# A hybrid decoder layer in split float32: weight chunks taken in pairs, and another order of the three partial products

## The chip, the cores and the metric

The kernel runs on one core of one Trainium2 chip. The metric is the device time of one execution in microseconds (us). An execution is also recorded by the profiler; the views quoted here come from that trace. Engines: TensorE (PE, its weight loads shown apart as PEld), VectorE (DVE), ScalarE (ACT), GpSimd (POOL) and SyncE (SP, which issues the weight transfers).

## The reference

One layer for 256 tokens of width 2048: half a SwiGLU, a token mixer, half a SwiGLU, each between two RMS norms. DEPTH is 1 and D_FF is 5504.

```python
def swiglu(x, w_gate, w_up, w_down):
    return (jax.nn.silu(x @ w_gate) * (x @ w_up)) @ w_down

f1 = swiglu(rms_norm(h, ffn1_pre_norm[l]), ffn1_w_gate[l], ffn1_w_up[l], ffn1_w_down[l])
h = h + 0.5 * rms_norm(f1, ffn1_post_norm[l])
m = hybrid_token_mixer(rms_norm(h, mix_pre_norm[l]), l, w_in[l], ..., w_out[l])
h = h + rms_norm(m, mix_post_norm[l])
f2 = swiglu(rms_norm(h, ffn2_pre_norm[l]), ffn2_w_gate[l], ffn2_w_up[l], ffn2_w_down[l])
h = h + 0.5 * rms_norm(f2, ffn2_post_norm[l])
```

The mixer multiplies its input by `w_in`, runs two gated linear attentions (GLA and HGRN2) on slices of the result, multiplies their outputs by two branch matrices, adds them under gates, and multiplies the sum by `w_out`. All arrays are float32.

## The kernel before, in words

**Products.** Tokens lie in two tiles of 128 (`NT`, index t); the contraction runs in k tiles of 128: 16 for a width of 2048 (`KT`), 43 for 5504 (`FKT`). Every float32 operand is split into a float32r part `hi` and a rest `lo`, and a product of two operands is three matmuls into one PSUM bank (`mm3`): hi*hi, then the activation's hi with the weight's lo, then the activation's lo with the weight's hi. The activation is the stationary operand (`xhi`, `xlo`, or `hkhi`, `hklo` in the second product of an FFN), the weight (`whi`, `wlo`, 512 columns) streams.

**Weight chunks.** `wchunk` brings 512 KB of a weight by one transfer on SP's queue into a tile `raw`, ACT writes `hi` (line 119), and DVE subtracts it from `raw` and writes `lo` (line 120). Tiles `raw`, `whi` and `wlo` have four buffers each, taken in turn, so the next transfer or split waits until the fourth one back is no longer read. Each engine takes its instructions in the order in which the tile framework laid them out. A chunk holds two k tiles by 512 columns in `gemm_block`, and one k tile by 1024 columns (half `hf` of the 2048) in `out_proj`; either is used for 12 matmuls.

**gemm_block** makes 512 columns for both token tiles. Without `held`, it takes a chunk, lays its products for t = 0 and t = 1, calls `side.pump()`, and goes on. The first block of each sublayer has `held`: there chunks are kept and token tile 1 follows as a whole; the change leaves that branch alone.

**out_proj** makes all 2048 columns in eight PSUM banks (four column blocks n by two t). The first four chunks are (k tile 0, half 0), (1, 0), (0, 1), (1, 1); then come half 0 and half 1 of each further k tile up to the last four (`TAIL`). Those last four give eight chunks at once, the four of half 0 in the ring and the four of half 1 in tiles `held`; they are used group by group, so that one (t, n) after the other is finished. `finish` then does the norm, the residual, and the next sublayer's transposed operand.

**Side work.** `Side.pump` lays one step of each waiting chain (transposes, attention, `finish`) between the products.

Of the kernel before, what the change touches and what calls it, by code (L numbers as in the profile page):

```python
# [16 lines left out]
D = 2048  # L17
NT = 2
# [13 lines left out]
class Side:  # L32
    """Chains of small steps whose instructions are laid between those of the large products.

    A light chain takes one step at every pump, the heavy ones take turns; a chain yields
    where the tensor engine would have to wait for what the other engines were just given."""

# [13 lines left out]
    def pump(self):  # L51
        for g in list(self.light):
            self._step(self.light, g)
        if self.heavy:
            g = self.heavy.pop(0)
            # two at a time take turns
            self.heavy.insert(min(1, len(self.heavy)), g)
            self._step(self.heavy, g)
# [12 lines left out]
def kernel(ctx: ExitStack, tc: tile.TileContext, a: dict, out: bass.AP):  # L71
    nc = tc.nc
    side = Side()
# [24 lines left out]

    # ------------------------------------------------------------------ weights
    def ring_alloc(w):  # L100
# [4 lines left out]
    def wchunk(src: bass.AP, w: int, alloc=ring_alloc):  # L105
        """src: [128, 2, w] of a weight in DRAM -> the float32r parts (hi, lo) of its two halves."""
        raw = ring.tile([P, 2, w], F32, tag="raw", name=nm("raw"))
        nc.sync.dma_start(raw, src)
        parts = alloc(w)
        if len(parts) == 1:  # L110
            split_into(*parts[0], raw)
            hi, lo = parts[0]
            return [(hi[:, i, :], lo[:, i, :]) for i in range(2)]
        for i, (hi, lo) in enumerate(parts):
            split_into(hi, lo, raw[:, i, :])
        return parts
# [5 lines left out]
    def mm3(ps, x, w, start, stop):  # L122
        (xhi, xlo), (whi, wlo) = x, w
        nc.tensor.matmul(ps, lhsT=xhi, rhs=whi, start=start, stop=False)  # L124
        nc.tensor.matmul(ps, lhsT=xhi, rhs=wlo, start=False, stop=False)  # L125
        nc.tensor.matmul(ps, lhsT=xlo, rhs=whi, start=False, stop=stop)  # L126

    def gemm_block(w_dram, c0, w, lhs, nkt=KT, held=None):
        """[256, w] of x @ W, one bank a token tile (two halves in two banks if w > 512). With
        held, the chunks after the ring's stay in its tiles, and token tile 1 comes after all  # L130
        of token tile 0."""
        nb = -(-w // CB)
        pss = [[ps_tile(f"mm{t}") for _ in range(nb)] for t in range(NT)]

        def chunk(k0, alloc):
            return wchunk(w_dram[k0 * P:(k0 + 2) * P, c0:c0 + w].rearrange("(k p) c -> p k c", p=P),
                          w, alloc)

        def mm(t, k0, parts):
            for i, part in enumerate(parts):  # L140
                kt = k0 + i
                x = lhs(t, kt)
                for j, ps in enumerate(pss[t]):
                    sl = slice(j * (w // nb), (j + 1) * (w // nb))
                    mm3(ps[:, :w // nb], x, (part[0][:, sl], part[1][:, sl]),
                        kt == 0, kt == nkt - 1)

        if held is None:
            for k0 in range(0, nkt, 2):
                parts = chunk(k0, ring_alloc)  # L150
                for t in range(NT):
                    mm(t, k0, parts)
                side.pump()
        else:
            kept = []
            for i, k0 in enumerate(range(0, nkt, 2)):
                kept.append((k0, chunk(k0, ring_alloc if i < 4 else held)))
                mm(0, *kept[-1])
                side.pump()
            for k in kept:  # L160
                mm(1, *k)
                side.pump()
            side.flush()
        return pss if nb > 1 else [ps[0] for ps in pss]

    # ------------------------------------------------------------------ helpers
    def load_bcast(name, after):
        """A row of 2048 on every partition, in four tiles; not before `after` is issued."""
        ts = []
# [7 lines left out]
    def rstd(ss, n, width, tag):  # L177
        """(ss / n + eps) ** -0.5 for ss [128, width]."""
        v = small.tile([P, width], F32, tag=f"{tag}v", name=nm("v"))
# [17 lines left out]
    def lhs_of(x):  # L197
        def lhs(t, kt):
            # the products are laid behind the transposes that they read
            side.until(lambda: x[2][t] > kt)  # L200
# [3 lines left out]
    def to_T(x, t, n, src):  # L204
        """src [128 tokens, 512] -> k tiles 4n.. of x's token tile t."""
        ps = ps_tile()
# [5 lines left out]
    def rstd4(ss, scale, tag):  # L212
        """rstd of rows of D whose squares' sums are in the four columns of ss; all but the
        last column is added up beforehand. scale: a power of two, into the result."""
        c = 1.0 / (D * scale * scale)
# [14 lines left out]
    def first_norm(t, x, rs, wcol):  # L230
        """x's token tile t = (h * w) transposed, the weights one channel a partition."""
        if t:
# [20 lines left out]
    def out_proj(w_dram, nkt, lhs, post, scale, pre, held, after):  # L253
        """acc = lhs @ W [256, 2048]; h += scale * rmsnorm(acc) * post; then the next
        sublayer's transposed operand (h * pre, and the rows' rstd, applied later), or the
        kernel's output."""
        acc = [[None] * 4 for _ in range(NT)]
        wpost = load_bcast(post, after)
        early, nxt, rs = [], None, [None, None]
        if pre is not None:  # L260
            # h * pre + rstd * acc * (post * pre): all but the second product ahead of time
            wpre = load_bcast(pre, after)
# [17 lines left out]
        for i, (kt, hf) in enumerate(order):  # L280
            parts = load(kt, hf)
            for t in range(NT):
                for n in (2 * hf, 2 * hf + 1):
                    mm(t, n, kt, parts)
            if i == 1:
# [12 lines left out]
        def finish(t, ss):  # L298
# [6 lines left out]
            if pre is None:  # L305
                # GpSimd takes one of the four
                for n in range(4):
# [46 lines left out]

    # ------------------------------------------------------------------ FFN
    def ffn(pre, x, rs, post, pre_next):
# [49 lines left out]

    # ------------------------------------------------------------------ mixer
    def mixer(x, rs):
        xl = lhs_of(x)
        w_in = a["w_in"]  # L410
        with ExitStack() as mctx:
# [11 lines left out]

            # masks of the small levels' pairs, four heads wide, and of the diagonal
            diag = mp.tile([P, P], U8, name="diag")
# [8 lines left out]

            # lower bounds of the HGRN forget gates: softmax over the two rows of logits,
            # one head a column
            lg = blk("lg")
# [34 lines left out]
            def transposed(src, dst):  # L472
                """A step later, dst = src with each 128 columns transposed."""
                yield
# [21 lines left out]
            def spawn_T(srcs, s):  # L496
                """Transposes of the two token tiles' blocks, a step later."""
                dsts = []
# [5 lines left out]
            def attention(t, qT, kT, fT, vs, gates, dv, br, b0):  # L504
                """Four heads of 128 key channels on token tile t; fT: the decays. kT holds
                each key times the decays after it in its block, qT each query times those up
                to it; from level to level the blocks double, and the pairs of a block's halves
                get their scores, as products of two factors in [0, 1]."""
                sc = blk("sc")
# [11 lines left out]
                for lv, c in enumerate(LEVELS):  # L521
# [11 lines left out]
                    else:  # L533
                        # the blocks' rectangles lie on the engine's own borders
                        for r0 in range(0, P, 2 * c):
# [99 lines left out]
            def gla_decays(code, fT):  # L635
                """exp(logsigmoid(code @ w + b) / 16), transposed; logsigmoid(y) as
                min(y, 0) - ln(1 + exp(-|y|))."""
                cs = blk("code")
# [76 lines left out]

            # ---- HGRN2, four heads at a time
            for g in range(2):
# [15 lines left out]

            # ---- gated merge
            ms = []
# [87 lines left out]
```

## Time and profile before

| | |
|---|---|
| time, median of 3 runs | 2231.12 us (2229.8 to 2231.39) |
| span of the profiled execution | 2230.0 us (no other time of that execution is given) |
| instructions | 26331 |
| mean granted TensorE clock | 0.997 |
| busy ACT, POOL | 45%, 3% |
| DMA | 410.24 MB, mean 184 GB/s |

The span runs from the first to the last instruction on the core. A timeline row gives start, duration, engine, line, operation, output from inputs, and in brackets the engine's idle time just before with the one it waited for. A matmul's duration is longer than the distance to the next one, since matmuls overlap; the distance of the starts is what counts. A wait row names engine, tile and line, what it waited for, the total in us, the number of times and the longest.

### The profile page before, as it was taken

Reading aid. Unit: us, or ns where it says so; the run is one execution under the profiler, and the core shown is the slowest. Engines: PE = TensorE matmul, PEld = TensorE weight load, DVE = VectorE, ACT = ScalarE, POOL = GpSimd, SP = SyncE. Lnnn points to the kernel's source line nnn. Section 1 sums busy time; section 2 is a strip of 40 time slices with the busy share of each in tenths; the row PEclk is TensorE's granted clock in tenths of the full one; section 3 lists DMA queues with packets and bytes.
Section 4 is the critical chain, followed back from the end, with each engine's and each line's share of the span. In section 5 each row is a group of like instructions: output and inputs, shape, how many; then the busy total and the mean of one; then the engine's idle time right before and its main releaser. Section 6 shows DMA issues by size and latency. Waiting matters only on the chain.

```text
span 2230.0 us, 26331 instructions
## 1 busy us (share of the span) xinstructions
PE 2203.5 (99%) x10197; PEld 1816.2 (81%) x10197; DVE 1183.0 (53%) x1278; ACT 995.1 (45%) x1202; POOL 69.1 (3%) x106
## 2 busy tenths in 40 slices
PE   8999999999999999999999999999999999999998
PEld 6888888898888788888888888878888888898886
DVE  5544444446555744657575656465444444445554
ACT  5444444444444564444434444355444444444443
POOL 0000000000000400000000000021000000000001
PEclk9999999999999999999999999999999999999999
DMA  7666666666666556655556775555666666666664
GB/s 233 186 187 185 189 186 185 189 200 205 190 192 196 159 171 189 170 148 145 155 154 174 232 204 185 183 171 177 188 189 186 184 188 189 170 217 190 191 193 135
DMA packets 189344, 410.24 MB, mean 184 GB/s; under 512 B 13681, under 2 KB 22289, under 8 KB 189218
## 3 DMA queue, kind: packets, MB, share of 16 engines
q1 hardware_dynamic: 183712, 400.21, 60.6%
q10 hardware_dynamic: 5506, 8.34, 1.2%
q8 instruction: 80, 1.31, 0.2%
q14 instruction: 46, 0.38, 0.0%
HBM read 406.41 MB, written 2.10 MB: 183 GB/s over the span
## 4 chain that ended last, share of the span: by engine, by line
PE 64%; DVE 1%; POOL 1%; ACT 0%; issue 0%; DMA 0%; POOLq 0%; ACTq 0%
PE mm L124 16%; PE mm L126 16%; PE mm L125 16%; PE acc L125 5%; PE acc L126 5%; PE acc L124 5%; PE ps L187 1%; PE ps L531 1%; PE ps L581 0%; PE ps L538 0%; POOL h L303 0%; PE ps L515 0%; DVE tmp L295 0%; DMA raw<-in_ffn_w_down_dram 0%; POOL v L218 0%
## 5 line engine op out<-in xcount | busy, mean ns | idle before, releaser
L120 DVE TENSOR_TENSOR wlo<-raw,whi 128x1024 fp32r<-128x1024 f32 (+2 forms) x740 | 898.4, 1216 | 889.3 <-ACT whi L119 888.3
L119 ACT ACTIVATE whi<-raw 128x1024 fp32r<-128x1024 f32 (+2 forms) x740 | 777.1, 1051 | 1072.5 <-PE mm L126 800.5
L124 PE MATMUL mm<-whi,xhi 128*128 128x512 f32 (+2 forms) x2096 | 817.0, 390 | 3.6 <-ACT whi L119 3.6
L125 PE MATMUL mm<-wlo,xhi 128*128 128x512 f32 (+2 forms) x2096 | 809.6, 386 | 5.0 <-DVE wlo L120 5.0
L126 PE MATMUL mm<-whi,xlo 128*128 128x512 f32 (+2 forms) x2096 | 810.0, 386 | 0.0
L125 PEld LDWEIGHTS mm<-wlo,xhi 128*128 128x128 f32 x2096 | 394.7, 188 | 84.6 <-DVE wlo L120 6.2
L124 PEld LDWEIGHTS mm<-whi,xhi 128*128 128x128 f32 x2096 | 394.2, 188 | 83.0 <-ACT whi L119 4.0
L126 PEld LDWEIGHTS mm<-whi,xlo 128*128 128x128 f32 x2096 | 394.0, 188 | 81.1 <-DVE xlo L120 0.7
L125 PE MATMUL acc<-wlo,hkhi 128*128 128x512 f32 x656 | 257.6, 393 | 0.3 <-DVE wlo L120 0.3
L124 PE MATMUL acc<-whi,hkhi 128*128 128x512 f32 x656 | 257.2, 393 | 0.5 <-ACT hT L376 0.5
L126 PE MATMUL acc<-whi,hklo 128*128 128x512 f32 x656 | 257.5, 393 | 0.0
L125 PEld LDWEIGHTS acc<-wlo,hkhi 128*128 128x128 f32 x656 | 123.2, 188 | 29.2 <-DVE wlo L120 1.3
L124 PEld LDWEIGHTS acc<-whi,hkhi 128*128 128x128 f32 x656 | 123.2, 188 | 28.7 <-ACT hT L376 1.0
L126 PEld LDWEIGHTS acc<-whi,hklo 128*128 128x128 f32 x656 | 123.1, 188 | 27.7
L217 POOL TENSOR_TENSOR v<-ss 128x1 f32<-128x1 f32 x12 | 6.3, 524 | 1691.7 <-ACT sq L228 1690.8
L124 PE MATMUL mm<-whi,oT 128*128 128x512 f32 x128 | 51.3, 401 | 0.0
L126 PE MATMUL mm<-whi,oT 128*128 128x512 f32 x128 | 50.7, 396 | 0.0
L125 PE MATMUL mm<-wlo,oT 128*128 128x512 f32 x128 | 50.6, 395 | 0.0
L119 ACT ACTIVATE hkhi<-hT 128x512 fp32r<-128x512 f32 (+1 forms) x44 | 26.9, 621 | 52.2 <-PE acc L125 52.1
L120 DVE TENSOR_TENSOR hklo<-hT,hkhi 128x512 fp32r<-128x512 f32 (+1 forms) x44 | 29.6, 679 | 31.0 <-ACT hkhi L119 31.0
L125 PE MATMUL acc<-wlo,xhi 128*128 128x512 f32 x112 | 44.1, 394 | 0.0
L126 PE MATMUL acc<-whi,xlo 128*128 128x512 f32 x112 | 44.0, 393 | 0.0
(196 smaller groups left out, 1145.0 us busy)
## 6 DMA issues: line engine op xcount, KB each, us to landing
raw<-in_ffn_w_down_dram SPq DMA_DIRECT2D x172, 512.0 KB, 4.5
raw<-in_w_in_dram SPq DMA_DIRECT2D x168, 512.0 KB, 3.8
raw<-in_ffn_w_gate_dram SPq DMA_DIRECT2D x160, 512.0 KB, 3.8
raw<-in_ffn_w_up_dram SPq DMA_DIRECT2D x160, 512.0 KB, 3.6
raw<-in_w_out_dram SPq DMA_DIRECT2D x32, 512.0 KB, 4.1
raw<-in_w_branch_gla_dram SPq DMA_DIRECT2D x16, 512.0 KB, 3.6
raw<-in_w_branch_hgrn_dram SPq DMA_DIRECT2D x16, 512.0 KB, 3.8
raw<-in_ffn_w_gate_dram SPq DMA_DIRECT2D x16, 384.0 KB, 3.3
```

The lines of the kernel that those rows point to most:

```text
L119: nc.scalar.activation(hi, src, AF.Copy)
L120: nc.vector.tensor_tensor(lo, src, hi.bitcast(F32), op=ALU.subtract)
L124: nc.tensor.matmul(ps, lhsT=xhi, rhs=whi, start=start, stop=False)
L125: nc.tensor.matmul(ps, lhsT=xhi, rhs=wlo, start=False, stop=False)
L126: nc.tensor.matmul(ps, lhsT=xlo, rhs=whi, start=False, stop=stop)
L187: nc.tensor.transpose(dst_ps[:, i * P:(i + 1) * P], src[:, i * P:(i + 1) * P], ident)
L217: nc.gpsimd.tensor_tensor(v[:, 0:1], ss[:, 0:1], ss[:, 1:2], op=ALU.add)
L531: nc.tensor.matmul(ps[:, i * 64:(i + 1) * 64], lhsT=kT[:, sl], rhs=halves(qT[:, sl])[1], start=True, stop=True)
```

## The change

Three edits. In `gemm_block` without `held`, two chunks are fetched together (four k tiles), and for each token tile the products go in the order of k tiles 2, 0, 1, 3: the second chunk's first k tile, both of the first chunk, the second chunk's other one. `side.pump()` is called after each token tile, as often as before. In `out_proj`, behind the first four chunks, the two halves of a k tile are fetched together, half 0 first, and half 1 is used first. In `mm3` the second and third matmul change places: hi*hi, the activation's lo with the weight's hi, then the activation's hi with the weight's lo. The output is the same sum in another order. Line numbers move by 3 to 10 behind line 136.

```diff
     def mm3(ps, x, w, start, stop):
         (xhi, xlo), (whi, wlo) = x, w
         nc.tensor.matmul(ps, lhsT=xhi, rhs=whi, start=start, stop=False)
-        nc.tensor.matmul(ps, lhsT=xhi, rhs=wlo, start=False, stop=False)
-        nc.tensor.matmul(ps, lhsT=xlo, rhs=whi, start=False, stop=stop)
+        nc.tensor.matmul(ps, lhsT=xlo, rhs=whi, start=False, stop=False)
+        nc.tensor.matmul(ps, lhsT=xhi, rhs=wlo, start=False, stop=stop)
...
         if held is None:
-            for k0 in range(0, nkt, 2):
-                parts = chunk(k0, ring_alloc)
-                for t in range(NT):
-                    mm(t, k0, parts)
-                side.pump()
+            for k0 in range(0, nkt, 4):
+                parts = chunk(k0, ring_alloc) + chunk(k0 + 2, ring_alloc)
+                for t in range(NT):
+                    for i, o in enumerate((2, 0, 1, 3)):
+                        one(t, k0 + o, parts[o], k0 + i == 0, k0 + i == nkt - 1)
+                    side.pump()
...
         for i, (kt, hf) in enumerate(order):
-            parts = load(kt, hf)
-            for t in range(NT):
-                for n in (2 * hf, 2 * hf + 1):
-                    mm(t, n, kt, parts)
+            if i < 4:
+                use = [(hf, load(kt, hf))]
+            elif hf == 0:
+                use = [(0, load(kt, 0)), (1, load(kt, 1))][::-1]
+            else:
+                use = []
+            for j, parts in use:
+                for t in range(NT):
+                    for n in (2 * j, 2 * j + 1):
+                        mm(t, n, kt, parts)
```

`one(t, kt, part, start, stop)` is the inner loop of the old `mm`, for one k tile. The three places at which the order of instructions is spoken of below follow.

PE in the steady work of the first FFN, before: one chunk (`whi_339`) for both token tiles (`mm0`, `mm1`).

```order
L124 MATMUL mm0_331_1774<-whi_339_1808,xhi0_2_99 128x512 [waits Activation_49]
L125 MATMUL mm0_331_1774<-wlo_340_1809,xhi0_2_99 128x512
L126 MATMUL mm0_331_1774<-whi_339_1808,xlo0_4_101 128x512
L124 MATMUL mm0_331_1774<-whi_339_1808,xhi0_2_99 128x512
L125 MATMUL mm0_331_1774<-wlo_340_1809,xhi0_2_99 128x512
L126 MATMUL mm0_331_1774<-whi_339_1808,xlo0_4_101 128x512
L124 MATMUL mm1_332_1775<-whi_339_1808,xhi1_3_100 128x512
L125 MATMUL mm1_332_1775<-wlo_340_1809,xhi1_3_100 128x512
```

The same block after: the pair's second chunk (`whi_345`) first, then the first one (`whi_342`).

```order
L124 MATMUL mm0_331_1774<-whi_345_1832,xhi0_2_99 128x512 [waits Activation_49]
L125 MATMUL mm0_331_1774<-whi_345_1832,xlo0_4_101 128x512
L126 MATMUL mm0_331_1774<-wlo_346_1833,xhi0_2_99 128x512 [waits DVE_49]
L124 MATMUL mm0_331_1774<-whi_342_1826,xhi0_2_99 128x512
L125 MATMUL mm0_331_1774<-whi_342_1826,xlo0_4_101 128x512
L126 MATMUL mm0_331_1774<-wlo_343_1827,xhi0_2_99 128x512
L124 MATMUL mm0_331_1774<-whi_342_1826,xhi0_2_99 128x512
L125 MATMUL mm0_331_1774<-whi_342_1826,xlo0_4_101 128x512
L126 MATMUL mm0_331_1774<-wlo_343_1827,xhi0_2_99 128x512
L124 MATMUL mm0_331_1774<-whi_345_1832,xhi0_2_99 128x512
```

The weight's `lo` part is now read third, and a token tile has three products of the second chunk, six of the first, and three of the second.

PE at the end of the first FFN's output product, before: the main loop's last chunk is `whi_987` (half 1, banks `acc02` to `acc13`), and the first of the last four k tiles is `whi_990`.

```order
L125 MATMUL acc13_725_3752<-wlo_988_5179,hkhi_984_5160 128x512
L126 MATMUL acc13_725_3752<-whi_987_5178,hklo_985_5161 128x512
L124 MATMUL acc00_708_3686<-whi_990_5196,hkhi_984_5160 128x512 [waits Activation_49]
L125 MATMUL acc00_708_3686<-wlo_991_5197,hkhi_984_5160 128x512 [waits DVE_49]
L126 MATMUL acc00_708_3686<-whi_990_5196,hklo_985_5161 128x512
```

The same place after: the main loop ends with `whi_982` (half 0, banks `acc00` to `acc11`).

```order
L125 MATMUL acc11_713_3702<-whi_982_5156,hklo_988_5167 128x512
L126 MATMUL acc11_713_3702<-wlo_983_5157,hkhi_987_5166 128x512
L124 MATMUL acc00_708_3686<-whi_990_5196,hkhi_987_5166 128x512 [waits Activation_49]
L125 MATMUL acc00_708_3686<-whi_990_5196,hklo_988_5167 128x512
L126 MATMUL acc00_708_3686<-wlo_991_5197,hkhi_987_5166 128x512 [waits DVE_49]
```

Half 0 of the main loop's last k tile, used 12 matmuls ahead of the end before, is now the last to be used.

ACT at the same place, before (the rows are the first halves of the splits; `whi_990` to `whi_999` are the four ring chunks of the last four k tiles, `held_1002` and on those of half 1).

```order
L119 ACTIVATE whi_982_5156<-raw_981_5154 128x1024
L119 ACTIVATE whi_987_5178<-raw_986_5176 128x1024
L119 ACTIVATE whi_990_5196<-raw_989_5194 128x1024
L119 ACTIVATE whi_993_5202<-raw_992_5200 128x1024
L119 ACTIVATE whi_996_5208<-raw_995_5206 128x1024
L119 ACTIVATE held_1002_5220<-raw_1001_5218 128x1024
L119 ACTIVATE whi_999_5214<-raw_998_5212 128x1024
L119 ACTIVATE held_1005_5226<-raw_1004_5224 128x1024
```

ACT there after.

```order
L119 ACTIVATE whi_982_5156<-raw_981_5154 128x1024
L119 ACTIVATE whi_985_5162<-raw_984_5160 128x1024
L119 ACTIVATE whi_990_5196<-raw_989_5194 128x1024
L119 ACTIVATE whi_993_5202<-raw_992_5200 128x1024
L119 ACTIVATE whi_996_5208<-raw_995_5206 128x1024
L119 ACTIVATE held_1002_5220<-raw_1001_5218 128x1024
L119 ACTIVATE whi_999_5214<-raw_998_5212 128x1024
L119 ACTIVATE held_1005_5226<-raw_1004_5224 128x1024
```

ACT's order does not move (half 1 of the last k tile is only numbered 985 instead of 987): `whi_996` takes the buffer of `whi_982`, `whi_999` that of `whi_985` (before: `whi_987`), and `held_1002` stands between them.

More of the change, by code (lines that the diff above doesn't have):

```diff
@@ L137, in chunk, with one @@
                           w, alloc)
+        def one(t, kt, part, start, stop):
+            x = lhs(t, kt)
+            for j, ps in enumerate(pss[t]):
+                sl = slice(j * (w // nb), (j + 1) * (w // nb))
+                mm3(ps[:, :w // nb], x, (part[0][:, sl], part[1][:, sl]), start, stop)
         def mm(t, k0, parts):
             for i, part in enumerate(parts):
[L141 to L146, printed above, removed]
+                one(t, k0 + i, part, k0 + i == 0, k0 + i == nkt - 1)
         if held is None:
-            for k0 in range(0, nkt, 2):
-                parts = chunk(k0, ring_alloc)
+            for k0 in range(0, nkt, 4):
+                parts = chunk(k0, ring_alloc) + chunk(k0 + 2, ring_alloc)
                 for t in range(NT):
-                    mm(t, k0, parts)
-                side.pump()
+                    for i, o in enumerate((2, 0, 1, 3)):
+                        one(t, k0 + o, parts[o], k0 + i == 0, k0 + i == nkt - 1)
+                    side.pump()
         else:
```

## The prediction

> **What bounds the kernel now.** I read the busy times first, then what the tensor engine (PE) waited for, then the cost of one split of a weight chunk, and last the timelines of the places at which PE waits.
>
> ```profile
> PE 2203.5 (99%) x10197; PEld 1816.2 (81%) x10197; DVE 1183.0 (53%) x1278; ACT 995.1 (45%) x1202; POOL 69.1 (3%) x106
> PE mm L125 <- DVE wlo L120: 5.0, 3, 2.0
> PE acc L125 <- DVE held L120: 0.8, 1, 0.8
> PE acc L125 <- DVE wlo L120: 0.3, 1, 0.3
> L120 DVE TENSOR_TENSOR wlo<-raw,whi 128x1024 fp32r<-128x1024 f32 x700 | 857.9, 1227 | 844.7 <-ACT whi L119 844.0
> L119 ACT ACTIVATE whi<-raw 128x1024 fp32r<-128x1024 f32 x700 | 741.5, 1060 | 1021.7 <-PE mm L126 753.4 <-PE acc L126 228.5 <-issue 13.8
> ```
>
> PE is busy for 2203.5 of 2230.0 us. The change issues the same products, so it can only move two things: the spacing of the matmuls, and the waits. There are about 26 us of idle time in all; the waits on `wlo` and `held` in the three wait rows make up 6.1 us of it. A split costs ACT 1.06 us and DVE 1.23 us, in that order, so a chunk is ready 2.3 us after ACT may start; ACT's own idle time is mostly a wait for PE to free a place in the ring. The spacing of the matmuls is seen in steady work, in the timeline of PE (below it, ACT's) in the first FFN:
>
> ```profile
> 251.51 0.39 PE L124 MATMUL mm<-whi,xhi 128*128 128x512 f32 x1
> ...
> 252.88 0.39 PE L124 MATMUL mm<-whi,xhi 128*128 128x512 f32 x1
> ...
> 254.24 0.40 PE L124 MATMUL mm<-whi,xhi 128*128 128x512 f32 x1
> ...
> 257.03 0.39 PE L124 MATMUL mm<-whi,xhi 128*128 128x512 f32 x1
> ...
> 251.71 1.06 ACT L119 ACTIVATE whi<-raw 128x1024 fp32r<-128x1024 f32 x1 [1.73 <-PE mm L126]
> 254.44 1.06 ACT L119 ACTIVATE whi<-raw 128x1024 fp32r<-128x1024 f32 x1 [1.67 <-PE mm L126]
> ```
>
> The rows at 251.51, 254.24 and 257.03 are the first products of three chunks. One chunk (12 products) takes 2.73 us, the next 2.79 us, and so in turn: 0.228 against 0.233 us a product, 5.52 us a pair. I read the alternation as one of the chunk's place in the ring, since a slow chunk has both token tiles in it as a fast one has, and ACT's split beside each is the same (251.71, 254.44).
>
> **Steady work.** In a pair of chunks the products now run in stretches of six from one chunk and six from the other, instead of twelve. Half the products stay fast and half slow, but the pace changes twice as often. The first six products of the fast chunk above take 1.37 us (251.51 to 252.88), the last six 1.36 us (to 254.24): a change of pace costs about 0.01 us, at the rows' resolution. With one more fast stretch in each of 268 pairs (168 of the two FFNs, 84 of the input product, 16 of the branches) that is 2.7 us; I take 2, with 0 and 5 for ends. By the Trainium skill ("TensorE: Matmul & The Clock Gate", Step-by-step: what each phase is for) streamed operand and weight load come through two independent ports, and a load takes nothing from a running matmul; by that the places in the ring could not matter, and this term would be 0 and the sum 2237.3. The two paces of the trace do not fit it.
>
> Does a pair come in time? It is split while PE uses the other pair in the ring. From the moment its places are free: 0.2 us to ACT's start (as in the tail below), 1.06 to the first `whi`, then two DVE splits of 1.23: 3.7 us, against 5.52 us of PE work. So 1.8 us are left where before three chunks (8.3 us) were ahead. That pays for one or two other steps of DVE, so I put the wait at 0 there. Raw chunks have more time: their place is free when DVE is done at 3.7, they land 4.5 us later (the median of the w_down transfers, row below), at 8.2, and are split two pairs on, at 11.0. Side steps are pumped as often as before, once in 12 products: 0. The cover is thinnest in the attention part of the mixer:
>
> ```profile
> 930.00:1160.00 230.00, 230.00 (x1252) 193.16 (x1251) 147.08 (x250) 97.60 (x146) 7.86 (x16) 1.00 0.53 150
> L120 DVE TENSOR_TENSOR wlo<-raw,whi 128x1024 fp32r<-128x1024 f32 x64 | 78.6, 1228 | 32.6 <-ACT whi L119 32.1
> ```
>
> The first row is the table by stretches (busy PE, PEld, DVE, ACT), the second the groups of DVE in the same stretch. In 230 us there are 32 pairs, 7.2 us each, because small products lie between. DVE has (147.1 - 78.6)/32 = 2.1 us of other work a pair, and 7.2 - 3.7 = 3.5 us for it. That is a mean; bunching is a rival below.
>
> **The end of each output product.** This is the term that decides. Ring places go round in order, four of each kind. The last four chunks that use the ring there (half 0 of the last four k tiles; I call them c1 to c4) take the places of the last two pairs of the main loop. T0 is the moment when the main loop ends, 717.18 in the first FFN. Timelines of ACT, DVE and PE:
>
> ```profile
> 714.64 1.06 ACT L119 ACTIVATE whi<-raw 128x1024 fp32r<-128x1024 f32 x1 [1.73 <-PE acc L126]
> 715.97 1.06 ACT L119 ACTIVATE held<-raw 128x1024 fp32r<-128x1024 f32 x1 [0.26 <-DMA raw<-in_ffn_w_down_dram]
> 717.38 1.06 ACT L119 ACTIVATE whi<-raw 128x1024 fp32r<-128x1024 f32 x1 [0.35 <-PE acc L126]
> 718.70 1.06 ACT L119 ACTIVATE held<-raw 128x1024 fp32r<-128x1024 f32 x1 [0.26 <-DMA raw<-in_ffn_w_down_dram]
> 721.68 1.06 ACT L119 ACTIVATE held<-raw 128x1024 fp32r<-128x1024 f32 x1 [1.92 <-DMA raw<-in_ffn_w_down_dram]
> 724.28 1.06 ACT L119 ACTIVATE held<-raw 128x1024 fp32r<-128x1024 f32 x1 [0.96 <-DMA raw<-in_ffn_w_down_dram]
> ...
> 715.74 1.23 DVE L120 TENSOR_TENSOR wlo<-raw,whi 128x1024 fp32r<-128x1024 f32 x1 [1.57 <-ACT whi L119]
> 717.06 1.23 DVE L120 TENSOR_TENSOR held<-raw,held 128x1024 fp32r<-128x1024 f32 x1
> 718.47 1.23 DVE L120 TENSOR_TENSOR wlo<-raw,whi 128x1024 fp32r<-128x1024 f32 x1 [0.18 <-ACT whi L119]
> ...
> 717.18 0.40 PE L124 MATMUL acc<-whi,hkhi 128*128 128x512 f32 x1
> ...
> 722.86 0.40 PE L124 MATMUL acc<-held,hkhi 128*128 128x512 f32 x1
> ```
>
> Before, c3 (whi at 714.64) takes the place of the last k tile's half 0, which PE left 2.76 us before T0; c4 (717.38) that of half 1, left at T0. The two PE groups on c1 to c4 take 5.68 us (717.18 to 722.86), 0.15 more than 24 products of 0.2305.
>
> After, half 0 is used last. So c3 may start only at T0 + 0.2, and c4, whose place is free early, stands behind c3 and the first `held` chunk in the queues of ACT and DVE, as before. Counted from T0:
> - ACT: c3 0.2 to 1.26. The first `held` chunk needs the raw place of c1, whose split moves too: its place is free at T0 - 5.5, DVE is done 0.2 + 1.06 + 1.23 later, at -3.0, and the transfer takes 4.5 (row below), so it lands at 1.5. ACT: held 1.5 to 2.56, c4 2.6 to 3.66.
> - DVE: c3 to 2.5, held 2.6 to 3.85, c4 to 5.1.
> - PE: c1 and c2 until 1.38, c3's hi*hi and lo*hi until 1.84, wait until 2.5, end 2.73; c4 from 3.66, its third product at 5.1. The group ends at 5.33 instead of 2.77 + 0.15: +2.4 us.
>
> ```profile
> raw<-in_ffn_w_down_dram SPq DMA_DIRECT2D x172, 512.0 KB, 4.5
> ```
>
> The delay is not recovered: the third and fourth `held` chunks wait for the raw places of c3 and c4, freed by DVE at 2.5 and 5.1 instead of -0.2 and 2.5. Before, they landed 4.7 and 4.6 us after that (721.68, 724.28); now at 7.2 and 9.7. The last is split at 9.7 + 2.29 = 12.0 instead of 9.4, and PE, which would need it at 10.6, waits for it: +2.6 there as well. Everything behind hangs on PE's end. Ends for one tail: 2.2 (DVE's chain alone, no late transfer) and 3.5 (a raw chunk 1 us later). The other two output products have the same order and rows, with T0 near 1464.9 and 2196.6 (0.2 us ahead of their c4):
>
> ```profile
> 1462.34 1.06 ACT L119 ACTIVATE whi<-raw 128x1024 fp32r<-128x1024 f32 x1 [1.67 <-PE acc L126]
> 1463.33 1.16 ACT L119 ACTIVATE held<-raw 128x512 fp32r<-128x512 f32 x2
> 1465.13 1.06 ACT L119 ACTIVATE whi<-raw 128x1024 fp32r<-128x1024 f32 x1 [0.65 <-PE acc L126]
> ...
> 2194.10 1.06 ACT L119 ACTIVATE whi<-raw 128x1024 fp32r<-128x1024 f32 x1 [1.73 <-PE acc L126]
> 2195.34 1.06 ACT L119 ACTIVATE held<-raw 128x1024 fp32r<-128x1024 f32 x1 [0.18 <-DMA raw<-in_ffn_w_down_dram]
> 2196.84 1.06 ACT L119 ACTIVATE whi<-raw 128x1024 fp32r<-128x1024 f32 x1 [0.44 <-PE acc L126]
> ```
>
> Three tails: 3 x 2.43 = 7.3 us, from 6.6 to 10.5.
>
> **The order of the three products.** `wlo` is read third, so at a place where PE waits for DVE's half one more product (0.23 us) runs first. The wait rows give five such waits, three on `mm` and two on `acc`: -1.1 us. At most that, at least 0. DVE's split now waits for PE itself, since `wlo` is read last; PE's last read of `wlo` lies 0.23 us behind that of `whi`, and ACT's 1.06 us cover it; what is queued behind on DVE is not later for it: 0. The start of the run and the first product of each sublayer keep single chunks.
>
> **Sum.** The profiled span is 2230.0 us and the median of the runs 2231.1, so 1.1 us lie around the span or between executions; I add to the median. 2231.1 + 2.0 + 7.3 - 1.1 = 2239.3 us.
>
> **Rivals.**
> *Absorbed.* Behind the first two output products PE waits again, for splits that stand behind DVE's end of the layer:
>
> ```profile
> 744.39 0.50 PE L125 MATMUL mm<-wlo,xhi 128*128 128x512 f32 x1 [2.05 <-DVE wlo L120]
> ...
> 746.32 0.39 PE L124 MATMUL mm<-whi,xhi 128*128 128x512 f32 x1
> ...
> 1490.82 0.51 PE L125 MATMUL mm<-wlo,xhi 128*128 128x512 f32 x1 [1.91 <-DVE wlo L120]
> ...
> 1492.36 0.63 PE L124 MATMUL mm<-whi,xhi 128*128 128x512 f32 x1
> ...
> 1494.92 0.52 PE L124 MATMUL mm<-whi,xhi 128*128 128x512 f32 x1
> ```
>
> If those waits do not move with PE's end, they swallow two of the tails: 2231.1 + 2.0 + 2.4 - 1.1 = 2234.4. Against it: DVE's work there starts from sums of squares of PE's own results. Chance 0.20.
>
> *Faster.* If the slow pace belongs to a long stretch on one chunk and not to its place, stretches of six could all run at the fast one: 268 x 0.06 = 16 us less, 2239.3 - 2.0 - 16 = 2221. It decides once 80 pairs (5 us) lose it and the tails cost less than I say. For it: the trace of before has no stretch of six in these products. Against it: the slow pace is there from the chunk's first products on (254.24 to 257.03). Chance 0.17, smaller gains of this kind among it.
>
> *Clock.* Behind the wait at 1490.82 six products take 2.56 us (1492.36 to 1494.92), 0.43 each, which costs 6 x 0.2 = 1.2 us and, with the two at its edges, some 1.5; behind the like wait at 744.39 eight products take 1.93 us (to 746.32), so there is no such drop. The waits of a new tail add up to 2.6 us within 5.3. If each draws such a drop: three tails and one more seam, +6, 2245. By the Trainium skill ("TensorE: Matmul & The Clock Gate", What's actually happening) the clock halves only after an idle window of about 3.4 us, which speaks against it; the drop after 1490.82 came from less idle time. Chance 0.08.
>
> *Thin cover.* If DVE's other work bunches in the attention part, each of the 32 pairs there waits 0.5 us: +16, 2255. Chance 0.08. That the change does something else than it says is excluded: the products stand in the new order.
>
> **Numbers.** The forecast has 0.47. 0.2% of 2231.1 is 4.5 us, about what a measurement of this kernel tells from no change: same is 2226.6 to 2235.6. Faster: 0.14 of the faster case. Same: its other 0.03, gains too small to tell, and the absorbed case, 0.23. Slower: 0.47 + 0.08 + 0.08 = 0.63. The range goes from 2228 (part of the faster case) to 2248, which leaves out the attention case and most of the faster one; the forecast's own range is 2236.6 (2231.1 + 0 + 6.6 - 1.1) to 2246.6 (2231.1 + 5 + 10.5 - 0).
>
> **What would show it.** In the profile after: waits of PE `acc` on `whi` and `wlo` of about 0.7, 0.9 and 1.4 us shortly after the end of each main loop, ACT's third split 0.2 us behind T0; in steady work no waits, and the pace changing every six products. I am wrong if the tails show no such waits, if `mm` rows wait on `wlo` in the mixer, or if the sum of PE's spacing over a pair is not near 5.53 us.

## The result, and the profile after

| | before | after |
|---|---|---|
| time, median of 6 runs each | 2231.26 us | 2238.72 us (2237.53 to 2242.38) |
| ratio | | 1.0031, 95% interval 1.0022 to 1.0041 |
| span of the profiled execution | 2230.0 us | 2235.9 us |

The change makes the kernel 0.3% slower. The forecast was 2239.3 us, so the time came out as said. The sum did not: its largest term is not there, and two that were put at nothing are. The profiled execution of the changed kernel is one of the faster of its six (spans from 2235.4 to 2240.2 us), so the 5.9 us between the two traces, which are taken apart below, are less than the 7.5 us between the medians; the other 1.6 us are in no trace.

The busy row of the page and the waits of PE, after (engine, line, what was waited for: total us, times, longest):

```profile
PE 2208.1 (99%) x10197; PEld 1816.6 (81%) x10197; DVE 1167.2 (52%) x1278; ACT 971.0 (43%) x1202; POOL 70.1 (3%) x106
PE mm L126 <- DVE wlo L120: 5.6, 5, 1.8
PE mm L124 <- ACT whi L119: 5.0, 2, 3.7
...
PE mm L124 <- ACT xhi L119: 0.7, 2, 0.4
PE acc L126 <- DVE held L120: 0.5, 1, 0.5
PE mm L125 <- DVE xlo L120: 0.2, 1, 0.2
```

PE is busy 4.6 us longer for the same 10197 instructions. No `acc` product waits for `whi` or `wlo` any more, where the forecast had its 7.3 us; `mm` products wait for `whi` once more than before.

Where the time goes is read by taking the n-th matmul of both timelines and following the distance of their starts:

| stretch (us, before) | growth of the distance | what lies there |
|---|---|---|
| start to 53 | +1.9 | first block |
| 53 to 492 | +0.4 | steady FFN products |
| 492 to 545 | -1.1 | start of the first output product |
| 697 to 742 | -0.7 | its tail |
| 742 to 792 | +0.4 | start of the mixer |
| 806 to 833 | +2.5 | the block behind the gate's code |
| 833 to 1247 | +1.2 | steady mixer products |
| 1247 to 1282 | +0.9 | a branch product |
| 1451 to 1536 | +0.3 | end of the mixer, start of the second FFN |
| 1536 to 1953 | +0.6 | steady FFN products |
| 2150 to the end | -0.6 | last tail |

The sum is +5.9 us, with small steps between. What makes the -1.1 at the start of the first output product stays open.

**Steady work.** Every sixth product of PE in the first FFN, after:

```profile
251.95 0.39 PE L126 MATMUL mm<-wlo,xhi 128*128 128x512 f32 x1
...
253.32 0.40 PE L126 MATMUL mm<-wlo,xhi 128*128 128x512 f32 x1
...
254.72 0.39 PE L126 MATMUL mm<-wlo,xhi 128*128 128x512 f32 x1
...
256.09 0.40 PE L126 MATMUL mm<-wlo,xhi 128*128 128x512 f32 x1
...
257.48 0.39 PE L126 MATMUL mm<-wlo,xhi 128*128 128x512 f32 x1
```

Six products take 1.37 and 1.39 to 1.40 us in turn, and a pair takes 5.53 us: the pace changes every six products, as forecast.

**The tail.** ACT and then PE at the end of the first output product, after:

```profile
715.51 1.06 ACT L119 ACTIVATE whi<-raw 128x1024 fp32r<-128x1024 f32 x1 [1.66 <-PE acc L125]
716.76 1.06 ACT L119 ACTIVATE held<-raw 128x1024 fp32r<-128x1024 f32 x1 [0.19 <-DMA raw<-in_ffn_w_down_dram]
718.30 1.06 ACT L119 ACTIVATE whi<-raw 128x1024 fp32r<-128x1024 f32 x1 [0.47 <-PE acc L125]
...
718.33 0.40 PE L124 MATMUL acc<-whi,hkhi 128*128 128x512 f32 x1
...
723.88 0.39 PE L124 MATMUL acc<-held,hkhi 128*128 128x512 f32 x1
```

T0 is 718.33. c3 is split at T0 - 2.8, not T0 + 0.2, and c4 at T0, as before the change. The two groups take 5.55 us (before: 5.68).

**The mixer.** ACT, then PE, then DVE in the block behind the gate's code, after:

```profile
802.85 2.00 ACT L119 ACTIVATE whi<-raw 128x1024 fp32r<-128x1024 f32 x2 [1.22 <-PE mm L125]
...
813.70 1.28 ACT L684 ACT_TABLE_LOAD   x1
...
815.63 1.05 ACT L119 ACTIVATE whi<-raw 128x1024 fp32r<-128x1024 f32 x1
...
817.19 2.94 ACT L119 ACTIVATE whi<-raw 128x1024 fp32r<-128x1024 f32 x3
...
818.28 0.50 PE L124 MATMUL mm<-whi,xhi 128*128 128x512 f32 x1 [1.31 <-ACT whi L119]
...
819.54 0.50 PE L126 MATMUL mm<-wlo,xhi 128*128 128x512 f32 x1 [0.52 <-DVE wlo L120]
...
816.71 1.23 DVE L120 TENSOR_TENSOR wlo<-raw,whi 128x1024 fp32r<-128x1024 f32 x1 [2.30 <-ACT whi L119]
```

The same stretch of ACT, before:

```profile
802.96 1.06 ACT L119 ACTIVATE whi<-raw 128x1024 fp32r<-128x1024 f32 x1 [1.87 <-PE mm L126]
...
810.84 1.04 ACT L119 ACTIVATE whi<-raw 128x1024 fp32r<-128x1024 f32 x1
...
815.77 1.04 ACT L119 ACTIVATE whi<-raw 128x1024 fp32r<-128x1024 f32 x1
```

In both, ACT is busy from 804 to 817 with the GLA decays and their table loads. Before, one split stands in the middle of them (810.84); after, none between 804.85 and 815.63. ACT stays away for 10.8 us. When it leaves, PE has two split pairs in hand; it ends them and stops at 816.97. By then the next pair's first chunk has its `hi` (815.63 + 1.05 = 816.68). But a pair's products begin with its second chunk (k tiles 2, 0, 1, 3), which ACT splits from 817.19 on, and PE goes on at 818.28. So the order within the pair is part of this stall. With the first chunk first, PE would have waited only for that chunk's `lo`, ready at 817.94: by these rows some 0.9 us instead of the two waits of 1.3 and 0.5 us. That is an estimate; no run tried it.

### The profile page after: what moved, and what is told of

Read it like the earlier page. It is cut to its first block, busy times and chain, and to the rows that moved or that the text cites. A ratio compares the mean times of both kernels' runs of the same rounds, so it can differ in the third digit from the quotient of the medians.

```text
span 2235.9 us, 26304 instructions
## 1 busy us (share of the span) xinstructions
PE 2208.1 (99%) x10197; PEld 1816.6 (81%) x10197; DVE 1167.2 (52%) x1278; ACT 971.0 (43%) x1202; POOL 70.1 (3%) x106
## 4 chain that ended last, share of the span: by engine, by line
PE 62%; DVE 2%; POOL 1%; ACT 1%; DMA 1%; issue 0%; ACTq 0%; POOLq 0%
PE mm L124 15%; PE mm L126 15%; PE mm L125 15%; PE acc L126 5%; PE acc L124 5%; PE acc L125 5%; PE ps L541 1%; PE ps L190 1%; DMA raw<-in_w_in_dram 1%; DVE tmp L305 0%; POOL h L313 0%; PE ps L591 0%; PE ps L548 0%; DVE wlo L120 0%; DVE held L120 0%
## 5 line engine op out<-in xcount | busy, mean ns | idle before, releaser
L120 DVE TENSOR_TENSOR wlo<-raw,whi 128x1024 fp32r<-128x1024 f32 (+2 forms) x740 | 880.5, 1215 | 879.8 <-ACT whi L119 873.2
L119 ACT ACTIVATE whi<-raw 128x1024 fp32r<-128x1024 f32 (+2 forms) x740 | 751.6, 1045 | 1019.7 <-PE mm L125 700.1
L381 DVE SCALAR_TENSOR_TENSOR hn<-mm,r,silu 128x512 f32<-128x512 f32 (+1 forms) x44 | 32.5, 739 | 43.6 <-PE mm L126 43.6
L395 ACT ACTIVATE silu<-mm,r 128x512 f32<-128x512 f32 (+1 forms) x44 | 29.5, 672 | 40.3 <-PE mm L126 37.2
L124 PE MATMUL acc<-whi,xhi 128*128 128x512 f32 x112 | 44.2, 394 | 0.0
```

What stands on the lines that cost most here:

```text
L119: nc.scalar.activation(hi, src, AF.Copy)
L120: nc.vector.tensor_tensor(lo, src, hi.bitcast(F32), op=ALU.subtract)
L381: nc.vector.scalar_tensor_tensor(hn[:, :w], u[:, :w], rs[t], s[:, :w], op0=ALU.mult, op1=ALU.mult)
L395: after = nc.scalar.activation(st[:, :w], g[t][:, :w], AF.Silu, scale=rs[t])
```

## The experiments

**The three edits one by one.** Each is one hunk of the change, put into the kernel before. The order of the products:

```diff
-        nc.tensor.matmul(ps, lhsT=xhi, rhs=wlo, start=False, stop=False)
-        nc.tensor.matmul(ps, lhsT=xlo, rhs=whi, start=False, stop=stop)
+        nc.tensor.matmul(ps, lhsT=xlo, rhs=whi, start=False, stop=False)
+        nc.tensor.matmul(ps, lhsT=xhi, rhs=wlo, start=False, stop=stop)
```

> The kernel before with the new order of the three products alone (hi*hi, lo*hi, hi*lo). Theory from the two traces: at the start the second product now needs xlo, which DVE makes behind other steps, so the first 20 us lose about 1.7 us; each wait on wlo elsewhere is 0.23 us shorter (about -1 in all). Together +0.3 to +1.2 us. Rival, the prediction's own step: only the shorter waits, -1.1 us, and a start as before.

Measured: 2231.69 against 2231.99 us, ratio 0.9999 (0.9990 to 1.0009). The distance grows by 1.9 us in the first 53 us and falls by 0.9 around 700 to 742 and by 0.7 between 1451 and 1536. PE at the start in this run:

```profile
10.45 0.63 PE L125 MATMUL mm<-whi,xlo 128*128 128x512 f32 x1
...
12.22 0.78 PE L126 MATMUL mm<-wlo,xhi 128*128 128x512 f32 x1
...
14.50 0.63 PE L125 MATMUL mm<-whi,xlo 128*128 128x512 f32 x1
...
15.64 0.66 PE L126 MATMUL mm<-wlo,xhi 128*128 128x512 f32 x1
16.13 0.39 PE L124 MATMUL mm<-whi,xhi 128*128 128x512 f32 x1
```

and before:

```profile
13.44 0.56 PE L125 MATMUL mm<-wlo,xhi 128*128 128x512 f32 x1
13.84 0.39 PE L126 MATMUL mm<-whi,xlo 128*128 128x512 f32 x1
```

The first block is reordered too. In the run with the new order, products stay at half pace (durations of 0.63) until 15.6 us; before, until 13.4. In the record of the granted clock the rise lies at 16.0 and at 13.8 us. That part is not the edit's: the run with gemm_block's pairs alone (next) keeps the old order, and its clock rises as late, at 15.9:

```profile
15.50 0.67 PE L125 MATMUL mm<-wlo,xhi 128*128 128x512 f32 x1
16.01 0.39 PE L126 MATMUL mm<-whi,xlo 128*128 128x512 f32 x1
```

That run has lost 1.1 us by 23 us. Over all runs of this case the rise lies between 12.6 and 16.0 us, with either order. With half of the later rise taken off (an estimate, since products run at half pace until then), the five runs with the new order in the first block have lost 0.7 to 1.3 us by 23 us, and the six others 0 to 0.2. So about 1 of the 1.9 us goes with the order and the rest with the moment at which the clock rose. The gain and the loss of this edit cancel. That the late `xlo` causes the loss is not shown: side transposes also move.

> The kernel before with pairs of chunks in gemm_block alone. Theory: pace changes twice as often, +2 us spread evenly over the FFN and mixer products, and the thinner cover shows at two places of the mixer: about +3 us near 816 us (ACT holds the pair's split back behind the decays' steps and table loads) and about +0.8 near 1268. Together +5 to +6.5 us. Rival: pace alone, +2 us, with the two stalls caused by the order of the three products or by out_proj instead.

```diff
-            for k0 in range(0, nkt, 2):
-                parts = chunk(k0, ring_alloc)
+            for k0 in range(0, nkt, 4):
+                parts = chunk(k0, ring_alloc) + chunk(k0 + 2, ring_alloc)
...
+                    for i, o in enumerate((2, 0, 1, 3)):
```

Measured: 2234.98 us, 1.0016 (1.0006 to 1.0025): +3.0, less than expected. The even growth is there (0.4 us over each FFN), and 0.6 near 1268; 1.1 us are the late rise of the clock at the start; the 2.5 us near 816 are not there (0.4), so the pairs alone do not make that stall. In this run the tile framework laid the decays in another order (ACT loads three tables there instead of five), and ACT comes back 2.1 us sooner:

```profile
810.99 1.28 ACT L677 ACT_TABLE_LOAD   x1
812.29 1.34 ACT L677 ACTIVATE fT<-m 128x256 f32<-128x256 f32 x4
813.53 1.99 ACT L119 ACTIVATE whi<-raw 128x1024 fp32r<-128x1024 f32 x2
```

> The kernel before with pairs of halves in out_proj alone. Theory: the pool gives a new chunk the place that was freed first, not the next one in turn, so half 1 first costs nothing at the tails; the waits there even shrink: -2 to 0 us. Rival, the prediction's main step: each of the three tails costs 2.4 us, +7.3 us, with waits of about 0.7, 0.9 and 1.4 us behind the end of each main loop.

```diff
...
+            elif hf == 0:
+                use = [(0, load(kt, 0)), (1, load(kt, 1))][::-1]
...
```

Measured: 2232.40 us, 1.0002 (0.9993 to 1.0011). The distance stays within 0.4 us all along. This refutes the forecast's main step.

**The places of the ring, strictly in turn.**

> The changed kernel, but the four places of whi and of wlo are fixed tiles that are taken strictly in turn. Theory (the prediction's step was wrong only in how places are given): now the last pair's half 0 does hold up a tail chunk at each of the three tails, PE waits there on whi or wlo again, 0.7 to 2.4 us a tail, so 2 to 7 us over the changed kernel. Rival: the tails do not care which place is taken, no wait there, same time as the changed kernel.

```diff
+    places = [[ring.tile([P, 2 * (16 + CB)], F32R, tag=f"{s}{i}", name=f"{s}{i}", bufs=1)
+               for i in range(4)] for s in ("whi", "wlo")]
+    taken = [0]
...
-        hi = ring.tile([P, 2, w], F32R, tag="whi", name=nm("whi"))
-        lo = ring.tile([P, 2, w], F32R, tag="wlo", name=nm("wlo"))
-        return [(hi, lo)]
+        i = taken[0] % 4
+        taken[0] += 1
+        return [tuple(p[i][:, :2 * w].rearrange("p (k c) -> p k c", k=2) for p in places)]
```

Measured: 2239.35 us, 1.0031 over before (1.0021 to 1.0041), as the changed kernel. The distance to the changed kernel grows by 0.7 us within the first tail and is 0.3 us smaller than before it at its end; in the other two it stays within 0.2. So with fixed places, too, a tail costs nothing. ACT's row in the first tail of this run:

```profile
714.64 1.06 ACT L123 ACTIVATE whi<-raw 128x1024 fp32r<-128x1024 f32 x1 [1.68 <-PE acc L129]
```

This split starts 2.8 us ahead of T0 (717.46 here), when c3's place is not yet free. It must be c4's, so the framework then lays c4's split ahead of c3's. The theory falls, the rival holds.

**Single chunks where ACT is away.** The changed kernel, with pairs everywhere but in two blocks (`single=True` takes the loop of the kernel before).

> The changed kernel, but the block of the gate's code and the block of GLA's keys behind it take single chunks as before. Theory: with three chunks of cover instead of one pair, ACT's 8 us of decay steps no longer stop PE near 816 us; the waits of 1.3 and 0.5 us there go, -2.6 us, about 2236 us. Rival: the place of the splits in ACT's order, not the cover, makes the stall, and it stays or moves: 0 to -1 us.

```diff
...
-            hq0 = gemm_block(w_in, O_CODE, 16 + CB, xl)
+            hq0 = gemm_block(w_in, O_CODE, 16 + CB, xl, single=True)
...
-            k = gemm_block(w_in, O_GK, CB, xl)
+            k = gemm_block(w_in, O_GK, CB, xl, single=True)
```

Measured: 2234.99 us, 1.0012 (1.0002 to 1.0021), 3.7 below the changed kernel's median (4.9 when each is taken against the kernel before of its own set). PE has no wait between 813 and 820 us, and the distance falls by 2.4 us there. ACT's row at the point in question:

```profile
809.76 1.04 ACT L119 ACTIVATE whi<-raw 128x1024 fp32r<-128x1024 f32 x1
```

The split stands among the decays again, and ACT still loads five tables. With single chunks a place comes free every 2.8 us, so that one can be free when that order is laid; this reading of the framework is argued. The rival is not fully excluded: cover and place of the split changed together. That pairs are needed for the stall is shown.

**The old order of products in the changed kernel.** The diff is that of the first experiment the other way round.

> The changed kernel with the old order of the three products (both pairings, hi*hi, hi*lo, lo*hi). Theory: costs add: +3.0 (pairs in gemm_block) + 0.4 (pairs in out_proj) over before, about 2235 us, no stall near 816 as with gemm_block's pairs alone; the stall of the changed kernel then needs the new order of products as well. Rival: the two pairings together make that stall, about 2238 us, and the order of products is worth nothing.

Measured: 2235.45 us, 1.0015 (1.0005 to 1.0024), as expected; the stall near 816 costs 0.5 us of distance. The three edits alone give -0.3, +3.0 and +0.4 us, 3.1 in all; all three together give 7.5. Of the 4.4 us between, the stall is about 2 (2.5 against 0.5); the rest is open. In this run ACT loads three tables at that place, as with gemm_block's pairs alone; with single chunks (before, and in the run with the new products alone) it loads five, and with pairs and the new products five. So the stall needs both the pairs and the order of ACT's steps with five loads.

**Where the two paces come from.** The forecast read the alternation as one of places. They are 4224 bytes apart, 33 x 128, so that every second one starts in the other half of a 256-byte line. The trace holds no addresses; halves are worked out here from the sizes of the tiles and the order of the pools in the kernel, taken to lie one behind the other. Only the placement is changed in the kernel before:

> The kernel before with another placement in SBUF and nothing else: places of the whi and wlo rings 4352 bytes apart instead of 4224, and 128 bytes of padding ahead of the tiles that the output products and the branches read, so that every streamed operand and every stationary one starts in the same half of a 256-byte line. Theory: the slow one of the two paces comes from a streamed operand whose bit 7 of the address differs from the stationary operand's; with none left, every product takes 0.2267 us, 740 chunks x (2.763 - 2.720) = -32 us at most, -20 at least. Rival 1: the pace goes with the turn of the chunks (or with ACT and DVE beside), not with the address: 0 us and the alternation stays. Rival 2: it goes with the place but the other way round: all slow, +25 us.

```diff
+    pad = work.tile([P, 32], F32, name="pad", bufs=1)
+    nc.vector.memset(pad, 0.0)
...
-        hi = ring.tile([P, 2, w], F32R, tag="whi", name=nm("whi"))
-        lo = ring.tile([P, 2, w], F32R, tag="wlo", name=nm("wlo"))
-        return [(hi, lo)]
+        pad = w if w <= CB else 544
+        hi = ring.tile([P, 2, pad], F32R, tag="whi", name=nm("whi"))
+        lo = ring.tile([P, 2, pad], F32R, tag="wlo", name=nm("wlo"))
+        return [(hi[:, :, :w], lo[:, :, :w])]
...
-    wrow = const.tile([KT, P], F32, name="wrow")
+    wrow = work.tile([P, CB], F32, tag="tmp", name=nm("wrow"), bufs=3)[:KT, :P]
```

(The last edit frees the space.) Measured: 2204.96 us, ratio 0.9882 (0.9867 to 0.9896), -27 us. Two places in turn, in PE's timeline:

```profile
251.53 0.39 PE L127 MATMUL mm<-whi,xhi 128*128 128x512 f32 x1
...
254.25 0.39 PE L127 MATMUL mm<-whi,xhi 128*128 128x512 f32 x1
...
256.96 0.39 PE L127 MATMUL mm<-whi,xhi 128*128 128x512 f32 x1
```

Both chunks take 2.72 us; the alternation is gone. The counter-test moves the same 128 bytes ahead of the rings (its diff is against the aligned kernel):

> The kernel before with the padding of the aligned run put ahead of the rings instead of behind them: streamed ring chunks lie in the other half of a 256-byte line than every stationary operand. Theory (bit 7 of the two addresses decides the pace): all ring products are slow, 12 x 0.2333 = 2.80 us a chunk instead of 2.76 on the mean, 740 x 0.037 = +27 us, about 2257, and no alternation. Rival (an even distance of the places is what helps, whatever the stationary operand's address): as fast as the aligned run, 2205.

```diff
+    padp = ctx.enter_context(tc.tile_pool(name="padp", bufs=1))
     ring = ctx.enter_context(tc.tile_pool(name="ring", bufs=4))
...
-    pad = work.tile([P, 32], F32, name="pad", bufs=1)
+    pad = padp.tile([P, 32], F32, name="pad")
```

Measured: 2248.69 us (two runs), 1.0073 (1.0053 to 1.0093), +16. The sign is the theory's, the size is not. The table by stretches, 60 to 460 us, of before, aligned and the counter-test (the first field behind the length is PE's busy time with its count of matmuls):

```profile
60.00:460.00 400.00, 400.00 (x1776) 327.03 (x1775) 187.15 (x163) 172.66 (x183) 0.00 (x0) 1.00 0.65 186
60.00:460.00 400.00, 400.00 (x1806) 332.43 (x1806) 190.56 (x167) 174.47 (x184) 0.00 (x0) 1.00 0.65 188
60.00:460.00 400.00, 400.00 (x1761) 325.38 (x1760) 186.22 (x164) 172.01 (x181) 0.00 (x0) 1.00 0.64 184
```

In the same time PE issues 1776, 1806 and 1761 products: +1.7% and -0.8%. So the even distance alone does not help; how the streamed operand lies to the stationary one does. The slow side is nearer to the mixed one: half way between the two extremes lies 2226.8 us, and the kernel before takes 5 us more. Part of this may be the changes of pace, which neither extreme has: at the 0.008 us a pair that the changed kernel pays for doubling them (2.2 us over 268 pairs), 370 pairs make 3 us, an estimate. The rest stays open.

**The changed kernel in the aligned placement.**

> The changed kernel with the placement of the run in which all operands lie in the same half of a 256-byte line. Theory: the term of 2 us for the more frequent change of pace is gone, the start and the mixer's stall stay: 4 to 5 us over the kernel before in that placement (2204.96), about 2209.5. Rival: the 2 us are not of the pace, and the distance is 6.7 us as without the placement, about 2211.7.

The edit is that of the aligned run. Measured: 2210.36 us, 5.4 above the aligned kernel before. The distance to that kernel does not grow at all in the steady products: +1.2 at 52 and at 484 us, +4.1 from 822 to 1232, +8.0 from 1518 to 2123. So the even growth of the changed kernel is the pace changing more often. The stalls are there. Near 816 the distance grows by 4.2: 2.5 by the stall itself, as without the placement, and 1.7 behind it, where the granted clock was 0.50 from 808.1 to 811.5 us of this run.

**The best of both.** The aligned kernel, with the new order of products everywhere but in the first block.

> The aligned kernel before with the new order of products everywhere but in the very first block. Theory: the new order's gain at the places where PE waits for wlo (-1.6 us after the start in the run with that order alone) without its loss at the start: 2204.96 - 1.6 = about 2203.4. Rival: those gains belong to where the stalls happen to lie, and are gone or moved in the faster kernel: 2204 to 2206.

```diff
...
+        rest = [(xhi, wlo), (xlo, whi)]
+        for i, (l, w2) in enumerate(rest if first[0] else rest[::-1]):
+            nc.tensor.matmul(ps, lhsT=l, rhs=w2, start=False, stop=stop and i == 1)
...
+        first[0] = False
```

Measured: 2203.88 us, 0.9873 (0.9857 to 0.9890) of before. The aligned kernel had 2204.96 in another set of runs, and the intervals overlap: the placement is what beats both kernels, and nothing is shown for the order on top of it.

## Why the prediction was right in its number and wrong in its sum

- **Steady pace, +2.0 forecast.** Measured 0.4 + 1.2 + 0.6 = 2.2 us of even growth, which the aligned changed kernel does not have. Right, and for the reason given: the pace belongs to the chunk's place and changes every six products. The rule of the Trainium skill set beside it ("TensorE: Matmul & The Clock Gate", Step-by-step: what each phase is for: two independent read ports, no bandwidth taken) would have left the placement without effect; the runs show 44 us between the aligned placement and the counter-test, so the measurement decides against reading it that way.
- **Tails, +7.3 forecast.** The three tails give -0.7, -0.2 and -0.6. The step that failed is "Ring places go round in order": the pool hands out the place that is freed first, so c3 takes that of half 1, free 2.8 us ahead of T0 (715.51), and c4 that of half 0 (718.30). With the places in turn it would have cost nothing either: c4 "stands behind c3" in ACT's queue only as long as c3's place is free first, and otherwise the order of ACT's splits adapts. The text on the kernel ("taken in turn") and the last sentence on the change (which buffers `whi_996` and `whi_999` take) are wrong in the same point. The -0.7 is not the pairs' either: with the halves of a k tile in pairs alone the distance hardly moves there, and with the new order of products alone it falls by 0.9.
- **Order of products, -1.1 forecast, at most.** The shorter waits are there: -1.6 us in the run with this edit alone. The sentence that the start keeps its single chunks was true, but its products are reordered. The first block lost 1.9 us, of which about 1.2 go with the order and 0.7 with a clock that rose later in that execution (15.2 against 13.8 us).
- **Cover of one pair, 0 forecast.** The working set 3.7 us against 5.5, looked for other steps of DVE, and took ACT to be there whenever places come free. Near 816 ACT is away for 10.8 us, and PE loses 2.5. Near 1268 PE loses another 0.9 us; ACT had waited 4.15 us for row transfers ahead of the splits there (that this is the cause was not tried):

```profile
1266.09 2.01 ACT L119 ACTIVATE whi<-raw 128x1024 fp32r<-128x1024 f32 x2 [4.15 <-DMA row<-in_ffn_pre_norm_dram]
```

  The attention part, named as the weakest place, has no wait.
- **The signs named.** Two of the three signs of being wrong came: the tails show no waits, and `mm` rows wait on `wlo` in the mixer (0.5 us at 819.54 and again at 1272.93). The third did not: a pair takes 5.53 us. The wait of 1.4 us named for c4 is a slip; the working gives 1.0 (from 4.1 to 5.1).
- **Clock.** None of the tails drew the drop that was a rival. In the profiled executions it came at the start of a sublayer, once in either kernel, so it cancels. Other runs have none (the old products in the changed kernel) or two (gemm_block's pairs alone). The table by stretches of before, then after (the field ahead of the DMA share is the granted clock):

```profile
742.00:745.40 3.40, 1.35 (x6) 0.88 (x6) 3.40 (x4) 3.13 (x10) 3.31 (x4) 1.00 0.02 5
745.60:749.00 3.40, 3.40 (x18) 2.79 (x17) 2.63 (x4) 0.00 (x0) 2.88 (x6) 1.00 0.77 219
1488.40:1491.80 3.40, 1.49 (x8) 1.04 (x7) 3.40 (x3) 3.21 (x10) 3.31 (x4) 0.99 0.00 0
1491.80:1495.20 3.40, 3.40 (x9) 2.61 (x9) 2.63 (x5) 0.59 (x1) 2.96 (x7) 0.50 0.96 303
...
742.20:745.60 3.40, 1.55 (x9) 0.98 (x8) 3.40 (x4) 3.33 (x10) 3.31 (x4) 1.00 0.00 0
745.60:749.00 3.40, 3.40 (x10) 2.62 (x9) 2.63 (x4) 0.00 (x0) 2.96 (x7) 0.50 0.75 199
```

In the changed kernel the pace gives 2.2 us, the first block 1.9, ACT's absences 3.4, the start of the first output product -1.1, the tails -1.5 and the starts of the later sublayers about 0.7, which is 5.6 of 5.9. A term of 7.3 that is not there, and terms of 5.3 that were put at 0, made the number good. That was luck.

## What to carry to other kernels

A pool need not hand out its buffers in turn: look up which buffer a tile got before pricing who waits for whom. Taking work in larger pieces makes places come free later and in lumps; what counts against the lead is the longest time that any engine of the chain is away, not its mean load. Using the piece first that is ready last, as this change does, takes away from the lead once more. When one engine is 99% busy, look at its spacing as well as its waits: here 128 bytes of placement gained 27 us, and the whole change moved 7.5.

## What the runs showed of the hardware

- A float32r product of 512 columns comes every 0.227 us when its streamed operand lies in the same half of a 256-byte line as the stationary one, and 0.232 to 0.233 us otherwise; a whole kernel of the one or the other differs by 44 us (2204.96 and 2248.69). That 128 bytes between the two operands decide is measured; that the fast case is the one of equal halves rests on addresses worked out from the kernel.
- Behind a stall of some 2 us in a sublayer's first products the clock was 0.50 for 3.4 us (745.6 to 749.0 after, 1491.8 to 1495.2 before). PE was busy in the 3.4 us ahead for 1.5 us, so the window was not idle throughout; 1.35 us of work in 742.0 to 745.4 of before drew no drop. The Trainium skill ("TensorE: Matmul & The Clock Gate", What's actually happening) has the clock at half after an idle window of about 3.4 us; the length agrees, but part-idle stretches were enough here.
- These drops lie on a grid. Counted from the rise at the start, the drop at 1491.8 before comes 1478.0 us later, 433 times 3.413 us, and the one at 745.6 after comes 730.4 us later, 214 times; the 14 drops in the middle of the runs of this case all lie on such a grid, to about 0.01 of a step. In the step of 3.41 us ahead of each, PE was busy for 1.4 to 1.6 us. The stretch from 742.0 to 745.4 is no such step; the step there ends at 744.2. Two steps with 1.5 and 1.6 us of work drew no drop (that one, and one near 1494 in the changed kernel with the old products), and why is open; all other steps had more work. So whether a stall of 2 us costs a half clock depends on where it falls in a step.
